# A hybrid attention, DeltaNet and expert layer: the GpSimd splits leave the projection, and the attention groups move ahead

## The chip, the cores and the metric

One core of a Trainium2 chip runs one launch of the whole layer. The time is the device time of the launch in microseconds (us); lower is better. Engines: PE = TensorE (matmul), PEld = its weight load, DVE = VectorE, ACT = ScalarE, POOL = GpSimd, SP = SyncE, whose queue (SPq) issues most DMAs. L12 is line 12 of the kernel before.

## The reference, cut to what matters

A layer over 1024 latent tokens and 256 context tokens with 1024 channels, float32. One input projection feeds two head groups; the result goes through an output projection, and then a routed mixture of experts.

```python
h = modulate(rmsnorm(x, norm1_w), sh1, sc1)                 # 1024 latent and 256 context tokens
aq, ak, av, dq, dk, dv, dz, db, da = split(h @ w_in)        # 512,128,128,512,512,512,512,8,8 columns
# A: attention, 8 query heads and 2 key heads of 64, RMS norm and 2-D rotary on q and k
p = softmax(q k^T / 8); att = p @ v                         # latent queries over all 1280 keys
# B: gated DeltaNet, 4 heads of 128, short conv of 5 on q, k, v, one scan per direction
a = tril(k_beta k^T * decay, -1); u, w = (I + a)^-1 [v_beta, k_beta e^g]
s = s e^gl + kd^T (u - w s);      o = q_dec s + (q k^T * decay) v_new
dn = rmsnorm(o_fwd + o_bwd, o_norm_w) * silu(dz)
x = x + g1 * (concat(att, dn) @ w_out)
x = x + g2 * experts(modulate(rmsnorm(x, norm2_w), sh2, sc2))   # 16 experts, each takes 128 tokens
```

## The kernel before, in words

Tokens are handled in 10 tiles of 128 (2 context, 8 latent). Products that need float32 accuracy are made from high and low halves: ScalarE rounds a block to the matmul format (the high half), another engine subtracts to get the low half, and TensorE makes three products.

**Order of the work.** `build` calls the stages one after another, but this text order is only a priority: a planner in the framework gives each engine and each DMA queue a fixed order of its own from modelled times, and on the chip every engine and queue then runs its own order strictly, waiting at the head for data and for buffers. Which buffers exist is set by pools: a `tile(..., name, bufs=n)` takes one of n buffers of that name, and a pool that is closed gives its memory to the pools opened after it. Generators (`prep`, `tick`) cut long side work into steps that are handed out between the steps of the main loop.

**Projection** (`in_proj`, L504). The columns come in 11 groups: keys and values with the gates, k, q and v of the DeltaNet (two groups each), the attention's queries aq (two), z (two). While one group is computed the weights of the next are loaded and split by `weights` (L414), two halves of 128x1024: ScalarE makes the high half (L426), VectorE the low half (L427), and from the group of the first aq on GpSimd the low half. k, q, v go through `conv_head` (five VectorE steps per head, L660 and L662, and L668) and `conv_tail`. `queries` (L630) copies a 128x256 tile of PSUM to a row buffer "zz" on ScalarE and stores it; `out_gate` (L618) makes z (1 + tanh(z / 2)) with a buffer "zt" (one) for the tanh and "zz" (two) for the result, on ScalarE and VectorE, and stores it. After the second z group `router_consts` (L1182) loads the router's weights and folds shift and scale in; its last step is a 128x16 copy out of PSUM (L1209).

Beside aq and z runs the side work `prep`: `gates` (L704), `dn_chunk` (L799) for each of the 10 token tiles, `dn_wave` (L849) and the rope. `dn_chunk` loads transposed keys and queries (kq, L804 and L806) and a row of cumulated log decays for all partitions (grow, L808); GpSimd subtracts the column of the same decays (L809, 128x1024); ScalarE makes decay tables of it, Relu (L815) and Exp (L816), two for a context tile and three for a latent one (28 in all); TensorE multiplies keys with keys and queries (L826, L828) into the two PSUM banks "d", VectorE applies tables (L830 to L835), GpSimd masks (L844) and the SP queue stores (L840, L847). `dn_wave` inverts up to 128 triangles of 32x32 on VectorE, 31 steps of two instructions (L865, L867), copies the result T transposed on ScalarE (L870), and stores both from ScalarE's queue (L871, L872); the first of three waves runs here, the others in the scan. The rope loads raw keys (L1028, one buffer) and splits them (`split_rope`, L465: L477 to L501).

**Attention and scan.** `att_open` (L1042) loads the split keys in three blocks of 4, 4 and 2 tiles (L1053; one name "PT4" with two buffers) and transposes them (L1057) into KTs. `dn_step` (L950) is one chunk of one direction of the scan, 20 in all; its loads are on the SP queue. `att_group` (L1088) is one of 16 groups (block j of 256 queries, head pair hp): scores (L1113), copies with the row minimum (L1116), exp (L1119), transposes in the two PSUM banks "t" (L1123, L1124), and the product with v (L1130). `att_q(j)` (L1065) makes the queries of block j: a raw load (L1039), `split_rope`, 16 transposes in the banks "t" (L1081) and their copies (L1082) into QT, which has two buffers. The loop runs two scan steps and then one group; block j + 1's queries are made at the head of group (j, 2), block 0's at the head of (0, 0). After the loop come the output weights (`out_weights`), the rest of the groups, the output projection with the router, and 16 experts.

Of the kernel before, what the change touches and what calls it, by code (L numbers as in the profile page):

```python
# [9 lines left out]
F32 = mybir.dt.float32  # L10
# [3 lines left out]
AF = mybir.ActivationFunctionType  # L14
# [19 lines left out]
P = 128  # L34
D = 1024
KT = 8
# [48 lines left out]
class Layer:  # L85
# [51 lines left out]
    def build(self):  # L137
# [13 lines left out]
        self.att_open()  # L151
        self.dn_open()
# [3 lines left out]
        self.credit = 0  # L156
        for st in range(NT):
            for d in range(2):
                self.dn_step(self.sp, st, d)
                self.tick(3)  # L160
            self.att_group(*ga.pop(0))
            if st == 7:
                self.close("wv")
        self.close("sp")
        self.prep, self.credit = self.out_weights(), 0
        self.att_group(*ga.pop(0))
# [247 lines left out]
    def weights(self, col0, n, extra=None, eng=None):  # L414

        nc, A = self.nc, self.A
        W = 2832
        n2 = n + (16 if extra else 0)
        hi = self.wp.tile([P, KT, n2], F32R, name="whi", tag="whi", bufs=2)
        lo = self.wp.tile([P, KT, n2], F32R, name="wlo", tag="wlo", bufs=2)  # L420
        for k in range(0, KT, 4):
            raw = self.wp.tile([P, 4, n2], F32, name="wraw", tag="wraw", bufs=2)
            nc.sync.dma_start(raw[:, :, :n], dram(A["w_in"], k * W + col0, [[KT * W, P], [W, 4], [1, n]]))
            if extra:
                nc.sync.dma_start(raw[:, :, n:], dram(A["w_in"], k * W + extra, [[KT * W, P], [W, 4], [1, 16]]))
            nc.scalar.activation(hi[:, k:k + 4], raw, AF.Copy)  # L426
            (eng or nc.vector).tensor_tensor(lo[:, k:k + 4], raw, hi[:, k:k + 4], op=ALU.subtract)  # L427
        return hi, lo
# [75 lines left out]
    def in_proj(self, first):  # L504
# [54 lines left out]
        for i, (nm, c0, h, extra) in enumerate(groups):  # L559
            if i + 1 < len(groups):  # L560
                W.append(self.weights(groups[i + 1][1], 256, eng=nc.gpsimd if i > 5 else nc.vector))
            hi, lo = W.pop(0)
            if nm == "v" and h == 0:
                for _ in ml:
                    pass
                self.close("m2")
                self.sN, self.sQ, self.sT = {}, {}, {}
                self.prep, self.credit = prep(), 0
                self.rope = self.rope_first()
            if nm == "aq" and h == 0:  # L570
                self.close("cp")
            if nm == "z" and h == 0:
                self.prep = itertools.chain(self.prep, self.rope)
            if nm == "a":
                self.keys(hi, lo)
            elif nm in "kqv":
                gi = "qkv".index(nm) * 4
                for x in range(2):
                    tail, last = last, self.conv_head(self.cp, nm, h + x, hi, lo, x * P, self.cw, gi + h + x)
                    if tail:  # L580
                        self.conv_tail(*tail)
                    if (nm, h + x) == ("v", 3):
                        self.conv_tail(*last)
                    next(ml, None)
                    if nm == "v":
                        self.tick(TV)
            elif nm == "z":
                self.out_gate(hi, lo, h)
                if h:
                    self.router_consts(self.wp)  # L590
            else:
                self.queries(hi, lo, h // 2)
            next(ml, None)
            next(ml, None)
        self.tick(1000)
        self.close("kp")
        self.close("pp")
# [20 lines left out]
    def out_gate(self, hi, lo, h2):  # L618
        nc = self.nc
        for t in range(NLAT):  # L620
            ps = self.bank("s")
            self.token_major(ps, t + NCTX, hi, lo, 0, 256)
            th = self.wp.tile([P, 256], F32, name="zt", bufs=1)
            nc.scalar.activation(th, ps[:, :256], AF.Tanh, scale=0.5)
            z = self.wp.tile([P, 256], F32, name="zz", bufs=2)
            nc.vector.scalar_tensor_tensor(z, th, 1.0, ps[:, :256], op0=ALU.add, op1=ALU.mult)
# [3 lines left out]
    def queries(self, hi, lo, g):  # L630
        nc = self.nc
        for t in range(NLAT):
            ps = self.bank("s")
            self.token_major(ps, t + NCTX, hi, lo, 0, 256)
            q = self.wp.tile([P, 256], F32, name="zz", bufs=2)
# [68 lines left out]
    def gates(self):  # L704
# [53 lines left out]
        v.tensor_copy(tot.rearrange("p c u -> p (c u)"), ps[:, 80:160])  # L758
        self.egc, self.ekd, self.egl = new("egc", k), new("ekd", k), new("egl", k)
# [39 lines left out]
    def dn_chunk(self, pp, c):  # L799
# [9 lines left out]
        nc.gpsimd.tensor_tensor(gr, gr, self.gc[:, c, :, None].to_broadcast([P, 8, P]), op=ALU.subtract)  # L809
        E = {}  # L810
        for key, d, sg in (("f", 0, 1.0), ("b", 1, -1.0), ("q", 0, -1.0)):
# [3 lines left out]
            nc.scalar.activation(e, gr[:, 4 * d:4 * d + 4], AF.Relu, scale=sg)  # L815
# [33 lines left out]
    def dn_wave(self, pp, w, units, v):  # L849
# [20 lines left out]
        nc.scalar.copy(Tt[:n], T[:n].rearrange("p i j -> p j i"))  # L870
        nc.scalar.dma_start(sT[0, :n], T[:n].rearrange("p i j -> p (i j)"))  # L871
        nc.scalar.dma_start(sT[1, :n], Tt[:n].rearrange("p i j -> p (i j)"))  # L872
# [169 lines left out]
    def att_open(self):  # L1042
# [7 lines left out]
        for t0, T in ((0, 4), (4, 4), (8, 2)):  # L1050
            s = tp.tile([P, 2048], F32, name="ksplit", tag="PT4", bufs=2)[:, :512 * T]
# [36 lines left out]
    def att_group(self, j, hp):  # L1088
# [3 lines left out]
        if (j, hp) == (0, 0):  # L1092
            self.att_q(0)
        if hp == 2 and j < 3:
            self.att_q(j + 1)
# [86 lines left out]
    def router_consts(self, pool):  # L1182
# [14 lines left out]
        rw = pool.tile([P, KT, NE], F32, name="rw")  # L1197
        nc.sync.dma_start(rw, dram(A["router_w"], 0, [[KT * NE, P], [1, KT * NE]]).rearrange("p (k e) -> p k e", k=KT))
        rb = pool.tile([P, KT, NE], F32, name="rwb")
# [508 lines left out]
```

## Time and profile before

| | us |
|---|---|
| median of 3 runs | 1571.92 (1571.24 to 1575.38) |
| the profiled execution, its own time | 1576.82 |
| span of its trace | 1575.1 |
| PE busy | 1453.7 (92%) |
| DVE busy | 1175.2 (75%) |
| ACT busy | 941.5 (60%) |
| POOL busy | 252.2 (16%) |

The projection ends at 411 us of the span, scan and attention run to about 880, the output stage to about 990, the experts to the end. Matmuls are pipelined, so a busy PE is not PE at its peak. PEclk is the granted clock of TensorE as a share of full speed, taken as a mean over a stretch. Idle time of an engine matters only where TensorE, or the chain to the end, waits for it.

### The profile page before, as it was taken

Reading aid. Unit: us, or ns where it says so; the run is one execution under the profiler, and the core shown is the slowest. Engines: PE = TensorE matmul, PEld = TensorE weight load, DVE = VectorE, ACT = ScalarE, POOL = GpSimd, SP = SyncE. Lnnn points to the kernel's source line nnn. Section 1 sums busy time; section 2 is a strip of 40 time slices with the busy share of each in tenths; the row PEclk is TensorE's granted clock in tenths of the full one; section 3 lists DMA queues with packets and bytes.
Section 4 is the critical chain, followed back from the end, with each engine's and each line's share of the span. In section 5 each row is a group of like instructions: output and inputs, shape, how many; then the busy total and the mean of one; then the engine's idle time right before and its main releaser. Section 6 shows DMA issues by size and latency. Waiting matters only on the chain.

```text
span 1575.1 us, 25623 instructions
## 1 busy us (share of the span) xinstructions
PE 1453.7 (92%) x9416; PEld 1177.5 (75%) x9416; DVE 1175.2 (75%) x2456; ACT 941.5 (60%) x1513; POOL 252.2 (16%) x230
## 2 busy tenths in 40 slices
PE   4999998987899998999899994999999999999996
PEld 1887787887778777887677663888888887777775
DVE  1824578698677686466666588899999998988886
ACT  1815454434376543556756442788887877777763
POOL 0000003323111112101400112011111211341001
PEclk7899999998999999899999997999999999999999
DMA  9356825777835456532333655889999999999991
GB/s 336 115 185 207 289 77 176 216 242 252 216 86 165 125 166 190 150 98 68 125 110 121 220 215 220 338 323 405 392 389 399 392 379 337 383 353 357 377 359 29
DMA packets 187049, 377.28 MB, mean 240 GB/s; under 512 B 47631, under 2 KB 124187, under 8 KB 159403
## 3 DMA queue, kind: packets, MB, share of 16 engines
q1 hardware_dynamic: 176320, 339.94, 61.3%
q0 software_dynamic: 7488, 29.36, 6.3%
q10 hardware_dynamic: 3115, 6.34, 1.0%
q8 instruction: 74, 1.21, 0.3%
q14 instruction: 52, 0.43, 0.1%
HBM read 321.91 MB, written 53.68 MB: 238 GB/s over the span
## 4 chain that ended last, share of the span: by engine, by line
PE 63%; DVE 16%; DMA 10%; ACT 5%; issue 3%; POOL 1%; SPq 1%; POOLq 0%; ACTq 0%; DVEq 0%
PE ps_m L1617 9%; PE ps_m L1612 8%; PE ps_m L1614 8%; PE ps_t L1130 4%; DVE elo L1599 4%; PE ps_a L1113 3%; PE ps_t L1123 3%; PE ps_s L442 3%; PE ps_s L444 3%; PE ps_s L443 3%; PE ps_d L976 1%; DMA woraw<-in_w_out 1%; PE ps_d L297 1%; PE ps_d L982 1%; PE ps_d L991 1%
## 5 line engine op out<-in xcount | busy, mean ns | idle before, releaser
L1599 DVE TENSOR_TENSOR elo<-eraw,ehi 128x2048 fp32r<-128x2048 f32 x102 | 229.2, 2285 | 16.1 <-ACT ehi L1588 16.0
L1588 ACT ACTIVATE ehi<-eraw 128x2048 fp32r<-128x2048 f32 x105 | 199.3, 1926 | 43.2 <-PE ps_m L1614 38.2
L1612 PE MATMUL ps_m<-ehi,xx 128*128 128x512 f32 x512 | 161.7, 397 | 2.2 <-ACT ehi L1588 2.2
L1614 PE MATMUL ps_m<-ehi,xx 128*128 128x512 f32 x512 | 159.5, 393 | 0.0
L1617 PE MATMUL ps_m<-elo,xx 128*128 128x512 f32 x512 | 139.6, 394 | 9.1 <-DVE elo L1599 8.9
L1116 DVE TENSOR_SCALAR_CACHE_REDUCE prob<-ps_a 128x416 f32<-128x416 f32 (+1 forms) x192 | 109.5, 596 | 26.5 <-PE ps_a L1113 16.3
L1599 DVE TENSOR_TENSOR elo<-fraw,ehi 128x2048 fp32r<-128x2048 f32 x51 | 115.6, 2287 | 12.4 <-ACT ehi L1588 12.3
L1617 PEld LDWEIGHTS ps_m<-elo,xx 128*128 128x128 f32 x512 | 94.7, 188 | 34.6 <-DVE elo L1599 15.8
L1674 POOL DMA_INDIRECT out_x<-ey,idx x16 | 70.9, 4430 | 291.0 <-DVE ey L1672 291.0
L1113 PE MATMUL ps_a<-kts,QT 128*128 128x416 f32 (+1 forms) x384 | 108.8, 389 | 4.2 <-DVE prob L1116 4.2
L1614 PEld LDWEIGHTS ps_m<-ehi,xx 128*128 128x128 f32 x512 | 96.4, 189 | 20.7 <-issue 0.2
L1612 PEld LDWEIGHTS ps_m<-ehi,xx 128*128 128x128 f32 x512 | 94.6, 189 | 22.7 <-ACT ehi L1588 4.1
L1124 ACT ACTIVATE PT<-ps_t 128x512 f32<-128x512 f32 (+1 forms) x192 | 93.5, 525 | 29.1 <-PE ps_t L1123 27.3
L1123 PE MATMUL ps_t<-consts,prob 128*128 128x128 f32 x640 | 100.8, 283 | 3.4 <-ACT PT L1124 1.7
L1588 ACT ACTIVATE ehi<-fraw 128x2048 fp32r<-128x2048 f32 x51 | 97.8, 1930 | 9.4 <-PE ps_m L1614 9.4
L434 PE MATMUL ps_s<-whi,hh 128*128 128x256 f32 (+1 forms) x336 | 98.8, 295 | 0.5 <-ACT zz L636 0.4
L1119 ACT ACTIVATE prob<-prob,mn 128x1280 f32<-128x1280 f32 x64 | 87.3, 1364 | 19.0 <-DVE mn L1118 18.3
L436 PE MATMUL ps_s<-whi,hl 128*128 128x256 f32 (+1 forms) x336 | 95.8, 289 | 0.2 <-DVE hl L411 0.2
L435 PE MATMUL ps_s<-wlo,hh 128*128 128x256 f32 (+1 forms) x336 | 95.9, 288 | 0.0
L442 PE MATMUL ps_s<-hh,whi 128*128 128x512 f32 (+1 forms) x256 | 95.5, 373 | 0.0
L444 PE MATMUL ps_s<-hh,wlo 128*128 128x512 f32 (+1 forms) x256 | 94.7, 370 | 0.0
L443 PE MATMUL ps_s<-hl,whi 128*128 128x512 f32 (+1 forms) x256 | 94.0, 367 | 0.0
(431 smaller groups left out, 3403.7 us busy)
## 6 DMA issues: line engine op xcount, KB each, us to landing
eraw<-in_w_up SPq DMA_DIRECT2D x38, 1024.0 KB, 8.1
eraw<-in_w_down SPq DMA_DIRECT2D x32, 1024.0 KB, 7.3
eraw<-in_w_gate SPq DMA_DIRECT2D x31, 1024.0 KB, 9.5
wmod<-in_w_mod SPq DMA_DIRECT2D x24, 1024.0 KB, 6.1
fraw<-in_w_down SPq DMA_DIRECT2D x21, 1024.0 KB, 7.0
fraw<-in_w_gate SPq DMA_DIRECT2D x16, 1024.0 KB, 8.0
fqraw<-in_w_gate SPq DMA_DIRECT2D x16, 1024.0 KB, 8.9
fraw<-in_w_up SPq DMA_DIRECT2D x14, 1024.0 KB, 8.4
```

The source lines that it names most:

```text
L434: self.nc.tensor.matmul(ps[:, :n], self.hh[:, k, ts], hi[:, k, a:a + n], start=st, stop=False)
L442: self.nc.tensor.matmul(ps[:, :n], hi[:, k, a:a + P], self.hh[:, k, ts], start=st, stop=False)
L443: self.nc.tensor.matmul(ps[:, :n], hi[:, k, a:a + P], self.hl[:, k, ts], start=False, stop=False)
L444: self.nc.tensor.matmul(ps[:, :n], lo[:, k, a:a + P], self.hh[:, k, ts], start=False, stop=en)
L1113: nc.tensor.matmul(ps[:, k0:min(k0 + 512, w)], QT[:, h, i], self.KTs[:, kv * 2 + x, ks], start=x == 0, stop=x == 1)
L1116: v.tensor_scalar(pr[:, c0:c0 + w], ps[:, :w], -1.0, 3e38, op0=ALU.mult, op1=ALU.min, accum_out=mn[:, y:y + 1])
L1123: nc.tensor.transpose(pt[:, x * P:(x + 1) * P], pr[:, (k0 + x) * P:(k0 + x + 1) * P], self.ident)
L1588: nc.scalar.activation(hi, raw, AF.Copy)
L1599: nc.vector.tensor_tensor(lo, raw, hi, op=ALU.subtract)
L1612: mm(banks[a], xh[:, q], hi[:, cs], start=q == 0, stop=False)
L1614: mm(banks[a], xl[:, q], hi[:, cs], start=False, stop=False)
L1617: mm(banks[a], xh[:, q], parts[q][1][:, cs], start=False, stop=q == KT - 1)
```

## The change

1. `weights` always splits on VectorE; the subtraction of `dn_chunk` on GpSimd is gone, and ScalarE's Relu takes the column as a bias, head by head (the negated column `ngc` is made once in `gates`).
2. In the projection a pool `zp` with four buffers "zz" is opened where the convolution's pool closes; `out_gate` needs no buffer of its own for the tanh. `router_consts` moves from behind the second z group to the head of the first query group, and keeps its two 128x128 tiles in two "zz" buffers.
3. `dn_wave` stores T and its transposed copy from the SP queue, and VectorE makes the copy.
4. In `att_open` the third block of split keys gets a buffer of its own name, "PT2", in the other pool.
5. Block 0's queries are made right after `att_open`; group (0, 0) stands ahead of the first scan step, and the group after the loop falls away, so each group stands one place further ahead; block 1's queries are made in group (0, 1), block j + 1's in (j, 0).

```diff
 build():
         self.att_open()
+        self.att_q(0)
         self.dn_open()
...
         self.credit = 0
+        self.att_group(*ga.pop(0))
         for st in range(NT):
             for d in range(2):
                 self.dn_step(self.sp, st, d)
...
         self.prep, self.credit = self.out_weights(), 0
-        self.att_group(*ga.pop(0))
         self.tick(16)
 weights():
-            (eng or nc.vector).tensor_tensor(lo[:, k:k + 4], raw, hi[:, k:k + 4], op=ALU.subtract)
+            nc.vector.tensor_tensor(lo[:, k:k + 4], raw, hi[:, k:k + 4], op=ALU.subtract)
 in_proj():
-                W.append(self.weights(groups[i + 1][1], 256, eng=nc.gpsimd if i > 5 else nc.vector))
+                W.append(self.weights(groups[i + 1][1], 256))
...
             if nm == "aq" and h == 0:
                 self.close("cp")
+                self.zp = self.open("zp")
+                self.router_consts(self.wp)
...
                 self.out_gate(hi, lo, h)
-                if h:
-                    self.router_consts(self.wp)
 out_gate():
-            th = self.wp.tile([P, 256], F32, name="zt", bufs=1)
-            nc.scalar.activation(th, ps[:, :256], AF.Tanh, scale=0.5)
-            z = self.wp.tile([P, 256], F32, name="zz", bufs=2)
-            nc.vector.scalar_tensor_tensor(z, th, 1.0, ps[:, :256], op0=ALU.add, op1=ALU.mult)
+            z = self.zp.tile([P, 256], F32, name="zz", bufs=4)
+            nc.scalar.activation(z, ps[:, :256], AF.Tanh, scale=0.5)
+            nc.vector.scalar_tensor_tensor(z, z, 1.0, ps[:, :256], op0=ALU.add, op1=ALU.mult)
 queries():
-            q = self.wp.tile([P, 256], F32, name="zz", bufs=2)
+            q = self.zp.tile([P, 256], F32, name="zz", bufs=4)
 gates():
+        self.ngc = new("ngc", k)
+        v.tensor_scalar(self.ngc, self.gc, -1.0, None, op0=ALU.mult)
 dn_chunk():
-        nc.gpsimd.tensor_tensor(gr, gr, self.gc[:, c, :, None].to_broadcast([P, 8, P]), op=ALU.subtract)
...
-            nc.scalar.activation(e, gr[:, 4 * d:4 * d + 4], AF.Relu, scale=sg)
+            off = self.ngc if sg > 0 else self.gc
+            for h in range(DH):
+                u = 4 * d + h
+                nc.scalar.activation(e[:, h], gr[:, u], AF.Relu, bias=off[:, c, u:u + 1], scale=sg)
 dn_wave():
-        nc.scalar.copy(Tt[:n], T[:n].rearrange("p i j -> p j i"))
-        nc.scalar.dma_start(sT[0, :n], T[:n].rearrange("p i j -> p (i j)"))
-        nc.scalar.dma_start(sT[1, :n], Tt[:n].rearrange("p i j -> p (i j)"))
+        nc.sync.dma_start(sT[0, :n], T[:n].rearrange("p i j -> p (i j)"))
+        v.tensor_copy(Tt[:n], T[:n].rearrange("p i j -> p j i"))
+        nc.sync.dma_start(sT[1, :n], Tt[:n].rearrange("p i j -> p (i j)"))
 att_open():
-            s = tp.tile([P, 2048], F32, name="ksplit", tag="PT4", bufs=2)[:, :512 * T]
+            s = (tw if T == 2 else tp).tile([P, 512 * T], F32, name="ksplit", tag=f"PT{T}", bufs=2)
 att_group():
-        if (j, hp) == (0, 0):
-            self.att_q(0)
-        if hp == 2 and j < 3:
+        if hp == (0 if j else 1) and j < 3:
             self.att_q(j + 1)
 router_consts():
-        rw = pool.tile([P, KT, NE], F32, name="rw")
+        rw, rb = (self.zp.tile([P, 2 * KT, NE], F32, name="zz", bufs=4)[:, :KT] for _ in range(2))
-        rb = pool.tile([P, KT, NE], F32, name="rwb")
```

## Rows read from the trace of the kernel before

**Rows 1.** Windows: stretch and length, busy us (instructions) by engine, PEclk, DMA share, GB/s.
```profile
256.80:268.40 11.60, 7.35 (x29) 6.11 (x30) 6.80 (x18) 7.26 (x13) 5.51 (x6) 0.71 0.66 198
298.60:308.00 9.40, 7.03 (x44) 6.89 (x44) 6.96 (x18) 3.26 (x7) 6.99 (x6) 0.82 0.58 182
349.60:371.00 21.40, 6.64 (x28) 5.45 (x29) 20.51 (x58) 10.13 (x17) 9.79 (x6) 0.60 0.72 249
411.30:425.80 14.50, 9.02 (x57) 7.75 (x58) 3.97 (x9) 5.32 (x10) 3.31 (x9) 0.88 0.73 219
425.80:613.00 187.20, 185.11 (x1866) 149.08 (x1865) 138.27 (x442) 108.16 (x232) 31.65 (x30) 1.00 0.52 145
613.00:640.00 27.00, 21.95 (x199) 18.77 (x199) 16.75 (x44) 10.56 (x24) 5.41 (x5) 0.75 0.54 160
```

**Rows 2.** Waits of PE, 225 to 440 us: total us, times, longest us.
```profile
PE ps_d L826 <- issue: 11.5, 1, 11.5
PE ps_d L828 <- DVE Eb L835: 4.3, 1, 4.3
```

**Rows 3.** Timeline of the SP queue: start us, us, engine, line, operation, out<-in.
```profile
356.23 0.37 SPq L1028 DMA_DIRECT2D sr_raw<-skr  x1
...
357.24 0.53 SPq L804 DMA_DIRECT2D kq<-skT  x1
...
419.49 0.40 SPq L1053 DMA_DIRECT2D ksplit<-sks  x1
...
604.20 0.42 SPq L1039 DMA_DIRECT2D sr_raw<-sq  x1
```

**Rows 4.** Waits of the SP queue, 225 to 440 us.
```profile
SPq L1028 <- DVE sr_b L496: 9.4, 1, 9.4
```

**Rows 5.** Timeline of DVE, S1 and S3, with one earlier row.
```profile
227.93 1.55 DVE L662 SCALAR_TENSOR_TENSOR cacc<-craw,cw,cacc 128x1284 f32<-128x1284 f32 x1
...
246.73 9.86 DVE L662 SCALAR_TENSOR_TENSOR cacc<-craw,cw,cacc 128x1284 f32<-128x1284 f32 x4
...
327.93 2.50 DVE L865 TENSOR_TENSOR Ttmp<-L,T 128x252 f32<-128x252 f32 x1
330.47 2.50 DVE L867 TENSOR_TENSOR T<-T,Ttmp 128x252 f32<-128x252 f32 x1
333.01 0.43 DVE L865 TENSOR_TENSOR Ttmp<-L,T 128x255 f32<-128x255 f32 x1
...
334.60 1.79 DVE L867 TENSOR_TENSOR T<-T,Ttmp 128x256 f32<-128x256 f32 x1
...
350.09 1.76 DVE L132 TENSOR_TENSOR rs_a<-rs_a,rs_h 128x8 f32<-128x8 f32 x1
...
352.09 2.30 DVE L482 TENSOR_TENSOR sr_raw<-sr_raw,rs_r 128x512 f32<-128x512 f32 x1
354.43 0.69 DVE L489 TENSOR_TENSOR sr_sp<-sr_raw,kcs 128x512 f32<-128x512 f32 x1
```

**Rows 6.** Groups of POOL by line, 225 to 425 us: busy us, mean ns | idle before.
```profile
L809 POOL TENSOR_TENSOR grow<-grow,g_gc 128x1024 f32<-128x1024 f32 x10 | 20.1, 2017 | 36.5 <-DMA grow<-sgc 36.4
L427 POOL TENSOR_TENSOR wlo<-wraw,whi 128x1024 fp32r<-128x1024 f32 x8 | 20.0, 2505 | 42.8 <-ACT whi L426 36.9 <-PE ps_t L691 6.0
```

**Rows 7.** Line 427 on DVE, whole span: ns min/median/max, first and last start.
```profile
L427 DVE TENSOR_TENSOR wlo<-wraw,whi x14: 1217/1221/1293, 37.0 to 213.1; 128x1024 fp32r<-128x1024 f32 x12, 128x1088 fp32r<-128x1088 f32 x2
```

**Rows 8.** Groups of ACT by line, 225 to 425 us.
```profile
L815 ACT ACTIVATE Ef<-grow 128x512 f32<-128x512 f32 x10 | 6.3, 628 | 20.5 <-POOL grow L809 12.5 <-DMA sN<-Ef 8.0
...
L696 ACT ACTIVATE cjunk<-ps_t 128x128 bf16<-128x128 f32 x8 | 2.2, 277 | 0.2
```

**Rows 9.** Timeline of PE in S5.
```profile
634.90 1.33 PE L1081 MATMUL ps_t<-consts,sr_sp 128*128 128x128 f32 x5 [0.27 <-DVE sr_sp L501]
```

**Rows 10.** Waits before the splits of L427, 0 to 960 us, all engines.
```profile
POOL wlo L427 <- ACT whi L426: 36.9, 3, 20.6
...
DVE wlo L427 <- ACT whi L426: 16.8, 3, 9.1
```

More of the change, by code (lines that the diff above doesn't have):

```diff
@@ L411, in hidden_out, with weights @@
             nc.vector.tensor_tensor(self.hl[:, k, t0:t0 + w], hf[:, :w], hi, op=ALU.subtract)
-    def weights(self, col0, n, extra=None, eng=None):
+    def weights(self, col0, n, extra=None):
         nc, A = self.nc, self.A
@@ L596, in in_proj @@
         self.close("kp")
+        self.close("zp")
         self.close("pp")
```

## The prediction, made before the changed kernel was run

> **What bounds the kernel now.** Most of the span is TensorE time, so I looked for the stretches between the projection and the output stage, which is all that the change touches, in which TensorE is not at work or works at the lower of its two clocks. First the busy time by stretch: in the scan from 425.8 to 613 us TensorE is busy 185.11 of 187.20 us at full clock [rows 1], and there nothing but less TensorE work could help. Five stretches are different [rows 1]. What each loses is its length less its busy time at the granted clock: S1 (256.8 to 268.4) 11.60 - 7.35 x 0.71 = 6.4 us; S2 (298.6 to 308) 9.40 - 7.03 x 0.82 = 3.6; S3 (349.6 to 371) 21.40 - 6.64 x 0.60 = 17.4; S4 (411.3 to 425.8, the seam to the attention) 14.50 - 9.02 x 0.88 = 6.6; S5 (613 to 640) 27.00 - 21.95 x 0.75 = 10.5. Together 44.5 us. The clock is part of it: a TensorE that has stood still comes back at 1.2 instead of 2.4 GHz for a while, so S3 has a mean of 0.60.
>
> Then TensorE's waits: in S1 the products of keys (L828) wait 4.3 us for VectorE's L835, in S3 those of L826 wait 11.5 us for what the profile calls "issue" [rows 2]. The second name misleads: the SP queue issued a key load of L826 (L804) only at 357.24 us, behind the load of the next raw keys (L1028) at 356.23 [rows 3], for which the queue had stood 9.4 us until VectorE was done with the old ones [rows 4]. So S3 is a late VectorE.
>
> Why it is late stands in its timeline [rows 5]. One step of the convolution takes 1.55 us at 227.93, but four take 9.86 at 246.73; two steps of the triangle inversion take 2.50 us each beside 0.43 for a larger one right after; L482 takes 2.30 beside 0.69 for the same shape after it. GpSimd, busy 5.51 of 11.60 us in S1 and 9.79 of 21.40 in S3 but 31.65 of 187.20 in the scan [rows 1], runs the splits of L427 there, 8 at 2.505 us, and the subtraction of L809, 10 at 2.017 [rows 6]. I read the slow VectorE steps as the two engines holding each other up.
>
> **The change part by part.** *GpSimd's 18 large operations go.* The eight splits of L427 move to VectorE, 8 x 1.22 = 9.8 us of work [rows 7]. The ten of L809 go into ScalarE's Relu as a bias, one call per head: 28 calls of 0.63 us become 112. No 128x128 Relu is in the trace; the nearest row is the Square of that size at 0.277 us [rows 8], so 112 x 0.277 - 28 x 0.63 = 13.4 us more on ScalarE if each is paid in full, and nothing if four run end to end like one. I take the upper end, the nearest row. ScalarE is busy 10.13 of 21.40 us in S3 [rows 1], so this counts only in the chain of a chunk: three tables cost 3 x (4 x 0.277 - 0.63) = 1.4 us more, the GpSimd step 2.0 less.
>
> The Trainium skill speaks against this trade (ScalarE: Activation LUTs, Rules for kernel authors): about 0.3 us for each ACTIVATE with a pointer as bias, plus 0.83 ns per element. By that, as an estimate, a table costs 4 x 0.41 - 0.73 = 0.9 us more, three cost 2.7, and a chunk's chain would be 0.7 us longer instead of 0.6 shorter, the sum about 1 us smaller. The 0.277 us of rows 8 is less than the page gives; the row decides.
>
> S1: the four convolution steps lose 9.86 - 4 x 1.55 = 3.7 us of slowness, but two splits (2.4) join VectorE here. The chain gains 1.3, and 0.6 from the tables; as the gap of 4.3 us is about halved the return at the low clock shortens too. I take 3.5 (bounds 0 and 6.4). S2 has no single late cause that the change removes: 1 (0 to 3.6). S3: VectorE's slow instructions ahead of L1028 lose 2 x (2.50 - 0.43) + (1.79 - 0.43) + (1.76 - 0.43) + (2.30 - 0.69) = 8.4 us, where L132 at 350.09 is set against a far larger step, so it is a lower bound [rows 5]. Against it come two splits, 2.4, and the transposed copy of T that leaves ScalarE; no VectorE row shows that copy, the split of the same size takes 1.22 [rows 7], I take 1.2. The key load comes 8.4 - 2.4 - 1.2 = 4.8 us sooner, and about 2 us of the second gap and the low clock go with it: 7 (0 to 17.4).
>
> *The row buffers and the router constants.* With four buffers the stores of z and of the queries hold ScalarE, VectorE and the SP queue less. I count this in S4 alone. There the first transposes wait until the last z rows and the router bias are through, and the third block of split keys is issued at 419.49 [rows 3], because it wants the first block's buffer. In a buffer of its own it can load with the others, and the seam needs its 9.02 us of busy time at clock 0.88 and little more. I take 5 of 6.6 (0 to 6.6). The loads of the constants, six DMAs on SP, and their few small VectorE steps move into the first query group, where they lie beside TensorE's products; without that cover they would cost a microsecond or two.
>
> *T's stores* move from ScalarE's to the SP queue, and T's first store waits there for VectorE: behind it stand key loads, raw rows and stores of z. I cost it at nothing, as the planner puts it where it expects T, and give it a rival below.
>
> *One group ahead, and queries in group 1.* S5 is a chain of the queries: their raw load is issued at 604.20 [rows 3] and their transposes run at 634.90 [rows 9], and the group at whose head they stand cannot transpose its own rows before them, as both use the two banks "t". The change moves them from group (1,2) to (1,0), and the next from (2,2) to (2,0). In the text the load still follows the loads of the scan steps just ahead of it, so I see no more lead for it than before: the stall moves and stays, 0 (from -10.5, when it comes twice, to +10.5).
>
> **Sum:** 3.5 + 1 + 7 + 5 + 0 = 16.5 us. The profiled execution took 1576.82 us, so it would be 1560.3; the median of the three runs is 1571.92, 4.9 below it, and gives 1555.4. I forecast **1555 us**. The expert stage starts that much sooner with its loads and keeps its length.
>
> **The rivals.** *A, two query stalls* (at (1,0) and (2,0)): 16.5 - 10.5 = 6 us gained, 1566. For it: the third chain, which fell into the end of the scan, now falls into its middle, and 30 us pass from load to transposes. Against: one group more lies ready as filling. 0.14.
>
> *B, the SP queue is held elsewhere:* T's store stands before the key loads, S3 stays as it is, 9.5 us gained, 1562.4. For it: L1028 did just that for 9.4 us [rows 4]. 0.12. The Trainium skill (DMA: Bandwidth & Descriptors, Issuing engines are not separate DMA queues) says that issuing from several engines saves only the sequencer's issue time, by which B is worth nothing; rows 4 show what an in-order queue costs when its head waits for data.
>
> *C, slower: VectorE waits where GpSimd did.* GpSimd stood 36.9 us in three waits for ScalarE's high half before a split [rows 10], and little was behind it. VectorE's queue holds the chunk products that free the "d" banks, z and the inversion; its own splits of the earlier groups waited 16.8 us in three [rows 10]. It decides from 17 us of such waits on the path; at all 36.9, 1571.9 - 16.5 + 36.9 = 1592. Against: the planner would place the splits where it expects the high half. 0.11.
>
> *D, better:* S3 closes almost wholly and the queries lead: 16.5 + 6 + 6 = 28 us or more, 1544 and below. 0.14. *E, no change:* the planner's new order, which no row shows, spends what the parts give, or leaves the text's moves without effect: 1572. 0.07.
>
> **How the numbers follow.** Forecast 0.42, A 0.14, B 0.12, C 0.11, D 0.14, E 0.07. A difference under 0.3%, 4.7 us, is about what a measurement of this kernel cannot tell from no change. Faster: the forecast, D, B and most of A, 0.78; same 0.10; slower 0.12. The range goes from 1533 (most of D; all five stalls gone would be 1527) to 1571 (A, B and half of E); C and the edges are left out.
>
> **What would show it.** Right: L865, L867 and L482 with no instruction over 1 us; TensorE's wait at L826 under 7 us; the third block of keys issued with the others; from the last z product to the first score under 10 us. S5: a stretch with a clock below 0.8 while the queries of (1,0) are made. Wrong: VectorE's waits before L427 over 15 us in sum (then C), or a TensorE wait that ends in a key load issued behind T's store (then B).

## The result, and the profile after

The changed kernel is slower: 1585.33 us, median of 7 runs (1581.33 to 1593.13), against 1572.95 for 7 runs of before, a ratio of 1.0076 (95% interval 1.0056 to 1.0095). The profiled execution took 1586.36 us, its span is 1584.6 (before: 1576.82 and 1575.1). Line numbers are now up to 5 higher.

Single lines of TensorE in the changed kernel (count: ns min/median/max, first to last start in us): L437 are the projection's products, L1116 the scores, L1614 the experts.

```profile
L437 PE MATMUL ps_s<-whi,hl x336: 278/283/574, 39.4 to 402.7; 128*128 128x256 f32 x128, 128*128 128x272 f32 x40
L1116 PE MATMUL ps_a<-kts,QT x384: 345/363/721, 419.2 to 873.4; 128*128 128x416 f32 x128, 128*128 128x448 f32 x64
L1614 PE MATMUL ps_m<-ehi,xx x512: 387/389/774, 995.9 to 1547.1; 128*128 128x512 f32 x171
```

Beside the same lines of before:

| us | before | after | difference |
|---|---|---|---|
| last product of z | 410.9 | 402.7 | -8.2 |
| first score | 425.6 | 419.2 | -6.4 |
| last score | 864.6 | 873.4 | +8.8 |
| first expert product | 986.6 | 995.9 | +9.3 |
| span | 1575.1 | 1584.6 | +9.5 |

The projection gained 8.2 us, the seam gave 1.8 back, and from the first to the last score it now takes 454.2 us, not 439.0: 15.2 lost. Behind that little changed.

Windows of the changed kernel (columns as in [rows 1]), then of the kernel before:

```profile
280.00:320.00 40.00, 31.19 (x223) 30.21 (x223) 25.14 (x61) 14.89 (x36) 3.37 (x4) 0.87 0.58 167
400.00:430.00 30.00, 20.71 (x166) 17.78 (x165) 19.40 (x62) 11.89 (x22) 5.61 (x11) 0.89 0.84 227
520.00:530.00 10.00, 10.00 (x87) 8.94 (x78) 5.00 (x16) 2.97 (x7) 0.00 (x0) 0.67 0.38 93
520.00:560.00 40.00, 33.89 (x289) 29.36 (x279) 29.63 (x95) 12.61 (x28) 4.19 (x4) 0.71 0.43 129
560.00:600.00 40.00, 33.89 (x263) 28.31 (x262) 31.80 (x82) 17.86 (x36) 7.43 (x7) 0.82 0.51 147
600.00:640.00 40.00, 39.59 (x407) 31.90 (x407) 28.82 (x94) 26.51 (x56) 6.21 (x5) 1.00 0.51 140
```

```profile
520.00:560.00 40.00, 39.47 (x381) 30.59 (x380) 29.91 (x97) 16.85 (x37) 5.29 (x5) 1.00 0.50 148
560.00:600.00 40.00, 39.22 (x411) 31.58 (x411) 28.88 (x94) 20.91 (x45) 7.45 (x8) 1.00 0.56 171
600.00:640.00 40.00, 34.95 (x327) 29.84 (x326) 25.11 (x70) 15.51 (x35) 7.49 (x7) 0.83 0.59 176
```

Loss is counted as in the prediction, length less busy time at the granted clock. From 520 to 640 us it is 12.3 before (0.5 + 0.8 + 11.0) and 28.5 after (15.9 + 12.2 + 0.4). Of the 28.5 only 12.6 are idle time; the rest is the clock. 3.3 of them lie from 520 to 530 us, ahead of what is told next: TensorE was busy all the time there, at a mean clock of 0.67 (1.00 before); what lowered it stays open.

What happened there, in the timelines of TensorE and of the SP queue (changed kernel; start us, us):

```profile
537.39 1.07 PE L1116 MATMUL ps_a<-kts,QT 128*128 128x416 f32 x4
...
571.12 1.92 PE L1086 MATMUL ps_t<-consts,sr_sp 128*128 128x128 f32 x8
...
575.00 1.27 PE L1126 MATMUL ps_t<-consts,prob 128*128 128x128 f32 x8
```

```profile
537.94 0.42 SPq L1044 DMA_DIRECT2D sr_raw<-sq  x1
```

The last scores lie at 537.39, the load of block 2's raw queries is issued at 537.94, and the queries' transposes (L1086) come 33.2 us later. For 36.5 us, 538.5 to 575.0, TensorE has no attention work, only the steps of the scan with their gaps. In the kernel before the chain from load to transposes is nearly as long, 30.7 us [rows 3, 9], but attention work went on until 619.1, 15 us behind the load, and its pause was 19.9 us. Its last attention products ahead of the transposes:

```profile
618.47 0.67 PE L1113 MATMUL ps_a<-kts,QT 128*128 128x448 f32 x2
```

TensorE's waits in the changed kernel, 240 to 420 us (total, times, longest), and the SP queue at the seam:

```profile
PE ps_a L1062 <- DMA ksplit<-sks: 7.2, 1, 7.2
PE ps_d L1209 <- DVE rwbs L1204: 6.9, 1, 6.9
PE ps_d L831 <- DVE rs_r L133: 2.9, 1, 2.9
```

```profile
301.28 0.67 SPq L1201 DMA_DIRECT2D zz<-in_router_w  x1
...
389.81 14.30 SPq L628 DMA_DIRECT2D sz<-zz  x5
404.29 0.37 SPq L1058 DMA_DIRECT2D ksplit<-sks  x1
405.53 1.99 SPq L628 DMA_DIRECT2D sz<-zz  x2
407.61 1.09 SPq L1058 DMA_DIRECT2D ksplit<-sks  x2
```

S3's 11.5 us [rows 2] are down to 2.9, but two waits are new: the router's constants (load at 301.28, product at 305.19) and the first split keys, issued at 404.29 behind five stores of z, 1.6 us after the last product of z. Before, that load was issued 5.0 us ahead of the last product:

```profile
405.88 0.37 SPq L1053 DMA_DIRECT2D ksplit<-sks  x1
```

In the projection VectorE's slow steps are gone (changed kernel). The convolution steps of [rows 5] take 1.60 us each, beside no GpSimd split, and up to 425 us no inversion step of L870 takes over 0.43, where before one took 2.50:

```profile
245.42 1.22 DVE L428 TENSOR_TENSOR wlo<-wraw,whi 128x1024 fp32r<-128x1024 f32 x1
246.56 4.80 DVE L663 SCALAR_TENSOR_TENSOR cacc<-craw,cw,cacc 128x1284 f32<-128x1284 f32 x3
```

```profile
L870 DVE TENSOR_TENSOR Ttmp<-L,T x31: 183/357/426, 307.9 to 350.0; 128x31 f32<-128x31 f32 x2, 128x60 f32<-128x60 f32 x2, 128x87 f32<-128x87 f32 x2, 128x112 f32<-128x112 f32 x2
```

### The profile page after: what moved, and what is told of

Read it like the earlier page. It is cut to its first block, busy times and chain, and to the rows that moved or that the text cites. A ratio compares the mean times of both kernels' runs of the same rounds, so it can differ in the third digit from the quotient of the medians.

```text
span 1584.6 us, 25718 instructions
## 1 busy us (share of the span) xinstructions
PE 1461.6 (92%) x9416; PEld 1188.7 (75%) x9416; DVE 1172.9 (74%) x2468; ACT 952.0 (60%) x1594; POOL 213.4 (13%) x212
## 4 chain that ended last, share of the span: by engine, by line
PE 65%; DVE 15%; DMA 9%; ACT 7%; issue 3%; POOL 1%; SPq 1%; POOLq 0%; DVEq 0%; ACTq 0%
PE ps_m L1619 9%; PE ps_m L1614 9%; PE ps_m L1616 9%; PE ps_t L1133 3%; PE ps_t L1126 3%; DVE elo L1601 3%; PE ps_a L1116 3%; PE ps_s L443 3%; PE ps_s L445 2%; PE ps_s L444 2%; PE ps_d L981 2%; PE ps_s L435 2%; PE ps_s L436 2%; PE ps_s L437 2%; PE ps_d L987 1%
## 5 line engine op out<-in xcount | busy, mean ns | idle before, releaser
L1601 DVE TENSOR_TENSOR elo<-eraw,ehi 128x2048 fp32r<-128x2048 f32 x102 | 228.9, 2283 | 15.4 <-ACT ehi L1590 15.3
L1614 PE MATMUL ps_m<-ehi,xx 128*128 128x512 f32 x512 | 161.5, 397 | 2.2 <-ACT ehi L1590 2.2
L1601 DVE TENSOR_TENSOR elo<-fraw,ehi 128x2048 fp32r<-128x2048 f32 x51 | 115.5, 2284 | 12.4 <-ACT ehi L1590 12.2
L1127 ACT ACTIVATE PT<-ps_t 128x512 f32<-128x512 f32 (+1 forms) x192 | 93.2, 525 | 33.2 <-PE ps_t L1126 31.8
L1614 PEld LDWEIGHTS ps_m<-ehi,xx 128*128 128x128 f32 x512 | 94.7, 189 | 22.7 <-ACT ehi L1590 4.1
L1116 PE MATMUL ps_a<-kts,QT 128*128 128x416 f32 (+1 forms) x384 | 108.0, 392 | 3.3 <-DVE prob L1119 3.3
L1122 ACT ACTIVATE prob<-prob,mn 128x1280 f32<-128x1280 f32 x64 | 87.1, 1362 | 19.9 <-DVE mn L1121 19.6
L437 PE MATMUL ps_s<-whi,hl 128*128 128x256 f32 (+1 forms) x336 | 98.6, 298 | 0.2 <-DVE hl L412 0.2
## 6 DMA issues: line engine op xcount, KB each, us to landing
fqraw<-in_w_gate SPq DMA_DIRECT2D x16, 1024.0 KB, 10.3
```

The costliest lines, as they stand in the source:

```text
L437: self.nc.tensor.matmul(ps[:, :n], self.hl[:, k, ts], hi[:, k, a:a + n], start=False, stop=en)
L1116: nc.tensor.matmul(ps[:, k0:min(k0 + 512, w)], QT[:, h, i], self.KTs[:, kv * 2 + x, ks], start=x == 0, stop=x == 1)
L1601: nc.vector.tensor_tensor(lo, raw, hi, op=ALU.subtract)
L1614: mm(banks[a], xh[:, q], hi[:, cs], start=q == 0, stop=False)
```

## The experiments

**Where the queries are made.** Each edit is to the changed kernel, but the second's to the kernel before.

```diff
 1: -        if hp == (0 if j else 1) and j < 3:
    +        if hp == 2 and j < 3:
 2: (before) -        if hp == 2 and j < 3:
             +        if hp == (0 if j else 1) and j < 3:
 3: build(), ahead of the loop over the scan steps, then behind it
    -        self.att_group(*ga.pop(0))
    +        self.att_group(*ga.pop(0))
```

> The changed kernel with one thing put back: the queries of block j+1 are made at the head of group (j,2) again (block 1's at (0,2), not (0,1)). Theory 1 (query stall): in the changed kernel the queries of block 2 are made at (1,0), where VectorE still has the second wave's inversion to do, and TensorE loses about 27 us between 520 and 600 us; at (1,2) it loses about 11 as in the kernel before. So the stretch 520 to 600 is at full clock again, a loss of 8 to 12 us comes behind the second wave's last step, and the time is 1570 (1565 to 1575). Theory 2 (group ahead): the scan is late because a group of attention stands ahead of it and each group stands one place further ahead; the time stays at 1582 to 1588, wherever the queries are made.

> The kernel before with one thing of the change alone: the queries of block 1 at (0,1) and of block j+1 at (j,0). Theory 1 (query stall): the stall at (1,2), about 11 us, goes and one comes at (1,0), where the second wave's inversion (528 to 588 us) is on VectorE; groups stand one place later here than in the changed kernel, so the inversion is further on, and the new stall costs 18 to 27 us: the time is 1583 (1579 to 1589). Theory 2 (group ahead): the move costs nothing without the group ahead, 1570 to 1575.

> The changed kernel with the group order of before: no group ahead of the first scan step, the extra group behind the loop again; the queries stay in groups (0,1) and (j,0). Theory 1 (query stall): the stall stays, TensorE loses 18 to 27 us around the head of (1,0), and the time is 1577 to 1588. Theory 2 (group ahead): the order of the groups was the cost; the scan ends some 15 us sooner and the time is 1565 to 1572.

Measured: 1 1575.57 us, 1.0011 (0.9988 to 1.0034); 2 1588.12, 1.0110 (1.0074 to 1.0147); 3 1592.77, 1.0130 (1.0099 to 1.0161). Theory 2 fell: without the group ahead the changed kernel is slower still, and the move of the queries alone makes the kernel before slower by 1.1%. Theory 1 has the direction of all three; 3 lies 5 us above its range, 1 just above.

Was the price that of the second wave's inversion on VectorE, as theory 1 had it, or of the order on TensorE? Two more runs:

```diff
13: chain (load, norm, rope) at (0,1) and (j,0) as in the change;
    transposes and copies cut off and put at (j,2), two groups later (block 1's one; block 0's at the head of (0,0))
+        if hp == (0 if j else 1) and j < 3:
+            self.att_q(j + 1)
+        if hp == 2 and j < 3:
+            self.att_qt(j + 1)
14: -        if hp == (0 if j else 1) and j < 3:
    +        if hp == 1 and j < 3:
```

> The changed kernel with the chain of a block's queries (load, norm, rope) left at the head of (0,1) and (j,0), and only the transposes and their copies two groups later, at (j,2). Theory 1a (the order on TensorE: the transposes stand ahead of a group's own work): the loss of 28 us between 520 and 600 us falls under 8, the time is 1570 to 1576. Theory 1b (VectorE is too full with chain and inversion, and the scan steps wait for it): 15 us or more of it stay, with no transposes in the stretch, and the time is 1580 to 1586.

> The changed kernel with the queries, chain and transposes, at the head of (j,1) for every block. In the changed kernel TensorE loses 28 us between 520 and 600 us with the queries at (1,0), and about 7 us between 560 and 640 with them at (1,2). If the price follows what is left of the second wave's inversion at that place, (1,1) lies between: a loss of 10 to 20 us, time 1576 to 1582. If only the place ahead of a block's first group is dear, (1,1) costs no more than (1,2): under 9 us, time 1572 to 1577.

Measured: 13 1567.10 us, 0.9969 (0.9946 to 0.9992); 14 1581.54, 1.0064 (1.0041 to 1.0086). Windows of 13, then of 14:

```profile
520.00:560.00 40.00, 39.81 (x402) 33.46 (x396) 29.67 (x109) 22.99 (x49) 4.17 (x4) 0.91 0.48 142
560.00:600.00 40.00, 37.49 (x388) 31.36 (x389) 36.32 (x102) 21.14 (x46) 10.69 (x8) 1.00 0.61 166
```

```profile
520.00:560.00 40.00, 39.44 (x399) 32.50 (x396) 31.43 (x105) 21.30 (x45) 5.21 (x5) 0.96 0.51 155
560.00:600.00 40.00, 33.16 (x261) 29.18 (x260) 31.03 (x86) 13.16 (x29) 8.87 (x7) 0.70 0.49 144
```

14 by itself came out as the inversion would have it (19.1 us lost, 1581.54). 13 decides: the chain stays in the middle of the inversion, its load at 538.58, VectorE is busier than in the changed kernel (36.32 of 40 us in the second window), and the loss is gone. Theory 1b fell, 1a holds, with a time 3 us under its range. Now these runs on one scale, from the timelines, for block 2, with run 4 from further below. The pause is the time from the last attention product ahead of the transposes to the first behind them:

| run | load issued | attention work until | transposes | attention resumes | pause | loss 520 to 640 | ratio |
|---|---|---|---|---|---|---|---|
| 13 | 538.58 | 587.6 | 587.87 | 593.0 | 5.4 | 6.5 | 0.9969 |
| 4 | 547.90 | 611.7 | 612.02 | 617.6 | 5.9 | 2.5 | 1.0043 |
| 1 | 577.65 | 595.9 | 606.39 | 610.6 | 14.8 | 7.4 | 1.0011 |
| before | 604.20 | 619.1 | 634.90 | 639.0 | 19.9 | 12.3 | 1 |
| 14 | 556.69 | 564.9 | 593.05 | 597.2 | 32.3 | 19.1 | 1.0064 |
| after | 537.94 | 538.5 | 571.12 | 575.0 | 36.5 | 28.5 | 1.0076 |
| 3 | 554.45 | 538.5 | 589.05 | 592.9 | 54.4 | 29.1 | 1.0130 |
| 2 | 551.49 | 541.7 | 585.84 | 592.0 | 50.3 | 27.4 | 1.0110 |

In all rows but 13 and 4 it is 28.7 to 36.4 us from load to transposes. What differs is the lead, the attention work that still lies behind the load's issue: 18 us in run 1, 15 before, 8 in 14, 0.5 after, and in 2 and 3 it ran out 10 and 16 us ahead of the load. In every row the pause is the time from load to transposes less the lead, and 4 to 6 us more until attention resumes. Run 4 bears this out with the queries left whole: its load is issued 64 us ahead of the transposes, attention work fills all of it, and there is no stall. TensorE loses half to four fifths of a long pause, since the scan's steps run on in it, and with no lead (after, 3, 2) the loss stays at 27 to 29 us however long the pause is. Some 3 us of the loss in after and 13 lie ahead of the load, from 520 to 530 or 540. Why the lead is shorter at an earlier group is not shown.

The inversion is the smaller part: beside it the chain is at most 6 us longer than before. The group ahead gives a lead of 0.5 us in place of -16 (after against 3), as the prediction's rival A said of it; in TensorE's loss that is 0.6 us, in the ratio 0.5%, so the rest of its worth lies elsewhere.

**Queries cut in two the other way**: chain at (j,2), transposes at (j+1,0).

> The changed kernel, with the making of a block's queries cut in two: raw load, norm and rope (VectorE, ScalarE, GpSimd) at the head of group (j,2), the transposes in the banks t only at the head of (j+1,0), two groups later. Theory 1 (the stall is TensorE's own order: transposes that stand ahead of the group's work wait for a chain of 25 to 33 us): with two groups between, no stretch of the scan falls under 38 of 40 us of TensorE's time, the 27 us of 520 to 600 come back and no 7 us are lost later: first output product at 795 to 803, time 1564 to 1572. Rival (VectorE simply has too much to do while the second wave runs): the chain costs the same wherever its transposes stand, and the time is as with the queries back at (j,2), 1572 to 1578.

Measured: 1580.64 us, 1.0035 (1.0010 to 1.0060). The loss of 520 to 640 falls to 8.0, but 640 to 720 loses 6.8 where the changed kernel lost 1.8. 1580.64 lies above both ranges; why the transposes at (j+1,0) come so late (654.29, for a load of 577.38) stays open. Part of what the scan gains is lost behind it: from the last score to the first expert product it is 127.8 us in 6 and 129.2 in 1, against 122.5 in the changed kernel. What holds it there is open too.

**The projection by itself.**

```diff
 4: attention as before (group order, att_q, buffers of the split keys)
 5: -        rw, rb = (self.zp.tile([P, 2 * KT, NE], F32, name="zz", bufs=4)[:, :KT] for _ in range(2))
    +        rw = pool.tile([P, KT, NE], F32, name="rw")
    +        rb = self.zp.tile([P, 2 * KT, NE], F32, name="zz", bufs=4)[:, :KT]
 9: 5, and the eight splits on GpSimd again
10: 5, and the subtraction of L809 on GpSimd again, one Relu for four heads
```

> The changed kernel with the whole attention as before (group order, where queries are made, one name for the buffers of the split keys): what is left of the change is the projection (splits, Relu with a bias, row buffers, router constants early) and T's stores on the SP queue. Theory 1 (query stall): the projection ends about 8 us sooner than before, as in the changed kernel, and the attention loses nothing new, so 1565 (1560 to 1569). Theory 3 (projection gives nothing in the end: its new waits and the seam eat it): 1570 to 1576.

Measured: 1578.07 us, 1.0043 (1.0022 to 1.0063), slower than both theories had it, although the last product of z comes at 398.6. The first score is at 445.8: block 0's load stands in the SP queue behind 30 loads of the scan and of a wave (410 to 425 us). In the kernel before, with the same order in the text, it was issued at 413.94, ahead of them; why the planner put it behind them here is not shown. The seam lost what the projection and the missing query stall had won, and the last score, at 863.8, is where it was before (864.6). The load (SP queue, run 4):

```profile
425.82 0.43 SPq L1075 DMA_DIRECT2D sr_sp<-sqs  x1
```

> The changed kernel, with the router's weights loaded into a tile of their own in the projection's pool, not into a row buffer of the pool that opens only when the convolution's pool closes (the product with the shift keeps its row buffer). Theory 3a: the 6.9 us for which TensorE waits at 298 to 305 us for the constants' last product comes from that late load; it goes, the products of the projection end 5 to 7 us sooner (396 to 398), and the time is 1579 (1576 to 1582). Theory 3b: the side work on VectorE (first the gates and tables, then rope and queries) sets the seam whatever TensorE does; the products end sooner, but the first score stays at 417 to 419 us and the time at 1582 to 1587.

> The kernel with the router's weights in a tile of their own, and the eight splits of the query and z groups on GpSimd again, as before the change; the decay subtraction stays in the Relu's bias. Theory 4a (the two engines held each other up through these splits): convolution and inversion steps on VectorE beside a split take several times their time again, and of the 15 us by which the last product of the projection came sooner (395.6 against 410.9) 6 to 10 go: 402 to 406. Theory 4b (the subtraction of the decays was the one that mattered, or VectorE's added 9.8 us of splits ate the gain): the end stays within 2 us of 395.6.

> The kernel with the router's weights in a tile of their own, and the decay subtraction of a chunk on GpSimd again with one Relu for four heads, as before the change; the splits stay on VectorE. Theory 4a (the splits were the cost): the projection's last product stays within 3 us of 395.6. Theory 4b (the ten subtractions of 2.0 us each held VectorE up too): it comes at 400 to 404. The Relu head by head: if it costs the chain of a chunk what the prediction took (1.4 us for three tables), undoing it gives no more than 1 or 2 us back.

Measured: 5 1582.63 us, 1.0043 (1.0024 to 1.0062); 9 1589.56, 1.0110 (1.0058 to 1.0162); 10 1585.38, 1.0065 (1.0042 to 1.0088). The last products in 5, 9 and 10, one kernel each:

```profile
L437 PE MATMUL ps_s<-whi,hl x336: 277/283/575, 40.4 to 395.6; 128*128 128x256 f32 x128, 128*128 128x272 f32 x40
```

```profile
L437 PE MATMUL ps_s<-whi,hl x336: 274/283/575, 40.6 to 405.7; 128*128 128x256 f32 x128, 128*128 128x272 f32 x40
```

```profile
L437 PE MATMUL ps_s<-whi,hl x336: 278/284/574, 41.8 to 401.8; 128*128 128x256 f32 x128, 128*128 128x272 f32 x40
```

By these traces the router's late load cost 7.1 us, the splits on GpSimd 10.1 and the subtractions 6.2. One trace is good to some 3 us: the last product lies between 398.6 and 405.4 in the eight traces that have the change's projection as it is, and between 391.2 and 397.6 in the five with the router's tile (5, 8, 11, 12, 15). So both of theory 4's parts hold, 10's by less, and their sum of 16.3 is near the 15.3 us between 410.9 and 395.6; the four row buffers were not tried by themselves. The time of 5 is theory 3b's, but its first score, 413.0, is not. How GpSimd's work holds VectorE up stands in the timelines of the two engines in 9:

```profile
327.78 5.27 POOL L428 TENSOR_TENSOR wlo<-wraw,whi 128x1024 fp32r<-128x1024 f32 x2 [22.74 <-ACT whi L427]
```

```profile
327.82 0.42 DVE L870 TENSOR_TENSOR Ttmp<-L,T 128x252 f32<-128x252 f32 x1
328.27 2.51 DVE L872 TENSOR_TENSOR T<-T,Ttmp 128x252 f32<-128x252 f32 x1
330.82 2.51 DVE L870 TENSOR_TENSOR Ttmp<-L,T 128x255 f32<-128x255 f32 x1
333.37 0.42 DVE L872 TENSOR_TENSOR T<-T,Ttmp 128x255 f32<-128x255 f32 x1
```

Two splits last from 327.78 to 333.05. In them VectorE finishes two steps, the second after 2.51 us, where a dozen of 0.42 us would fit, and the next takes 2.51 again. The Trainium skill (SBUF — State Buffer, SBUF: two separate sides) calls this an exclusive lock on a pair of ports, held for a whole instruction; the trace agrees, 2.51 us for 0.42.

**The seam.** Run 7 is run 1 with the split keys' loads on GpSimd's queue; 8 takes 5, 6 and that queue together; 11 is 8 with `zp` on the other side of the memory; 12 is 8 with T's copy and stores on ScalarE again.

```diff
 7: -            nc.sync.dma_start(s, self.sks[t0:t0 + T].rearrange("t p i d -> p t i d"))
    +            nc.gpsimd.dma_start(s, self.sks[t0:t0 + T].rearrange("t p i d -> p t i d"))
11: -                self.zp = self.open("zp")
    +                self.zp = self.open("zp", side="right")
```

> The changed kernel with the queries at (j,2), as in the first experiment, and the three loads of the split keys issued from GpSimd's queue, which is free there, instead of the SP queue, where they stand behind stores of z. Theory 3c (the seam is the SP queue's order): TensorE's wait of 7.2 us for the split keys behind the last z product falls under 3 us, the first score comes at 412 to 415 instead of 419, and the time is 4 to 6 us under that of the first experiment, 1568 to 1572. Rival (the seam is memory that the projection frees only at its end, or VectorE): the loads cannot start sooner, the wait stays over 5 us and the time at 1573 to 1578.

> The changed kernel with all three: the router's weights in a tile of their own, the queries' transposes two groups behind their chain, the split keys loaded from GpSimd's queue. If the three causes add: 3 to 6 us for the router's wait, 15 to 20 for the query stall, 4 to 6 for the seam, less what the output stage gives back: 1556 to 1566. If the seam and the output stage are set by other engines than TensorE, only the query stall's part shows: 1566 to 1573.

> The best kernel so far (router tile, queries cut in two, split keys from GpSimd's queue), with the pool of the four row buffers on the other side of the memory, so that the split keys' first buffer no longer lies where the rows of z do. Theory 3d (the seam waits for memory: GpSimd's key loads waited 22.7 us until a store of z had read its row): the loads start before 398 us, the gap between the last z product and the first score falls from 17.7 to under 12 us, and the time is 4 to 7 us lower, 1559 to 1563. Rival (other tiles of the projection, the rope's above all, lie there too, or TensorE then waits for the queries' load): the gap stays at 15 to 19 us and the time at 1564 to 1568.

> The best kernel so far, with T's transposed copy on ScalarE and T's two stores on ScalarE's queue again, as before the change. Rival B of the prediction (T's store on the SP queue holds key loads and stores of z): the projection or the scan get 3 to 7 us shorter. Theory 5 (it costs nothing where it stands, since the planner puts it where T is ready): within 3 us of the best kernel, 1563 to 1569.

Measured: 7 1575.96 us, 1.0004 (0.9984 to 1.0024), the rival's time; 8 1566.08, 0.9948 (0.9912 to 0.9984); 11 1570.40, 0.9975 (0.9948 to 1.0003); 12 1569.20, 0.9970 (0.9946 to 0.9994). 11 and 12 cannot be told from 8. The traces of 7 and 11 are of executions of 1565.08 and 1561.87 us, 11 and 9 us under the medians. In 7 GpSimd's key loads waited 22.68 us, by the profile for a store of z (timeline of GpSimd's queue, run 7):

```profile
403.34 2.50 POOL L1058 DMA_DIRECT2D ksplit<-sks  x3 [22.68 <-DMA sz<-zz]
```

Theory 3c fell: the queue's order hid another wait. That it is for memory, run 11 bears out: with z's rows on the other side the first load waits no more for a store but for TensorE's last product (391.2), and is issued at 391.8:

```profile
391.78 0.94 POOL L1058 DMA_DIRECT2D ksplit<-sks  x1 [21.15 <-PE ps_s L437]
```

TensorE's longest wait from 395 to 425 us in 11 is then another:

```profile
PE ps_t L1091 <- DMA sr_sp<-sqs: 8.5, 1, 8.5
```

That load, of block 0's split queries, was issued at 392.90, behind four stores of z. The first score stays at 416.2 (415.3 in 8), and the gap from the last product to it grows from 17.7 to 25.0 us, more than either forecast had. So what holds the seam changes from run to run (stores of z, memory, the load of the split queries), and taking one away moves it little.

**The two costs taken out together**: 13 with the edit of 5.

> The changed kernel with the two edits that removed a cost by themselves, and no other: the transposes of the queries at (j,2) with their chain left where the change put it, and the router's weights in a tile of their own. By the two ratios against the kernel before (1.0076 to 0.9969 for the first, 1.0076 to 1.0043 for the second) it is 0.9936 if both add, 1562 us (1558 to 1567); the products of the projection end at 395 to 399 us and the scan loses under 9 us of TensorE's time between 520 and 640. If the seam is VectorE's, as the late first score of the experiment with the rows on the other side says, the second edit is worth little on top of the first: 1565 to 1569.

Measured: 1558.39 us, median of 6 (1554.99 to 1560.84), 0.9903 (0.9879 to 0.9927): faster than both kernels, by 1.0% than before. Products end at 392.6, first score 409.3, loss from 520 to 640 2.9 us. The second edit was worth no less than by itself.

## Why the prediction was wrong

The step that failed is **S5**, priced "0 (from -10.5, when it comes twice, to +10.5)". It lost 16.2 us (12.3 to 28.5), outside its bounds, all but 3.3 of them in one stall. The prediction saw that the load follows the loads of the scan steps and concluded that there was no more lead than before. But it took the old stall's loss as the price of a query chain, when that loss was what 15 us of attention work behind the load had left of a chain of 31. It needed the last attention product ahead of 634.90, which it did not look for; with it, a place without lead means a pause of the whole chain, 36.5 us here, of which TensorE lost some 25. Rival A came nearest by place, (1,0), but there was no second stall: at (2,0) 64.5 us lie between load and transposes, and 640 to 720 lost 1.8.

**S4**, priced 5, gave -1.8 us; from the last z product to the first score it is 16.5 us, not under 10. The third block of keys was issued with the others, as said; but while the products ended 8.2 us sooner, the first load came only 1.6 us sooner (404.29 for 405.88), as it stood behind stores of z, and by runs 7 and 11 in their memory.

**S2 and the router's constants**: "beside TensorE's products", a microsecond or two at worst; they cost 7.1, since their load waited for the row buffers' pool and their product stood in TensorE's order ahead of the queries' products.

**S1 and S3** were right in kind and too small: with S2 11.5 predicted, 15.3 measured without the router's wait. Two of the prediction's signs came out here: no slow inversion step in the projection, and 2.9 us of wait at L826's products (L831 now). The splits on VectorE take 1.218 us each, as taken. The Relu, changed kernel (busy us, mean ns):

```profile
L820 ACT ACTIVATE Ef<-grow,g_ngc 128x128 f32<-128x128 f32 x40 | 13.0, 391 | 14.4 <-DMA grow<-sgc 7.6 <-DVE Qb L835 3.9 <-DVE cacc L663 1.7
```

A table of four heads takes 13.0 / 10 = 1.30 us instead of 0.63, 0.67 more; the row of 0.277 us [rows 8] had given 0.48, too little by 0.19. By the Trainium skill (ScalarE: Activation LUTs, Rules for kernel authors) the prediction's estimate was 0.9, too much by 0.23. In the time it cannot be seen by itself: run 10 undoes it together with the subtraction, and its interval overlaps that of 5.

**The sum**, with the projection split by run 5's trace: -15.3 + 7.1 + 1.8 + 15.2 + 0.5 (last score to first expert) + 0.2 = +9.5 us of span, where 16.5 less was predicted. Rival C, the only one on the slow side, did not happen: the eight splits on VectorE waited 0.9 us between 240 and 420. Rival B neither: with T's stores on ScalarE's queue again (12) nothing is gained. D's time, 1544 and below, came in no run: with the queries leading and the router's tile, run 15 is at 1558.39, near the forecast's 1555 by another way.

## What to carry to other kernels

Here the pause that a chain caused in an in-order engine's work was the chain's length less the work that the engine's order still had between the chain's start and its end, and a few microseconds to resume. Move the start and the end as two separate things, and price a new place by that lead, not by what the old place lost. When a stretch gets shorter, look at what is issued next, through which queue and into whose memory, because the seam behind it need not move. Taking GpSimd's work away from beside VectorE was worth about 15 us of the projection here, and a single late constant at the head of an order took 7 back.

## What was not expected

TensorE's clock made the pause dearer than its idle time. In the changed kernel from 540 to 560 us TensorE was busy 15.62 of 20 us with scan steps and the granted clock was 0.60, so mostly the lower of its two levels (1.2 of 2.4 GHz); of 28.5 us lost 16 are the clock's. Loads from GpSimd's queue landed 8.5 to 11.6 us after their issue in run 7 and 4.8 to 10.3 in 11; of the same loads from the SP queue in the changed kernel one has a landing on record, 5.7 us. What else the DMA engines moved then was not held equal.
